# Moving the elementwise part of a chunked recurrence behind its projections, and splitting each unit of it in two

## The chip, the cores and the metric

The kernel runs on one core of one Trainium2 chip. The metric is the device time of one execution in microseconds. The core's engines are TensorE (PE in the profile), VectorE (DVE), ScalarE (ACT), GpSimd (POOL) and SyncE (SP, which here only issues DMAs). Each works through its own instructions strictly in the order in which they were laid down, and waits on semaphores for the others.

## The reference

A network of two blocks on 1024 tokens of width 1024. The change lies in the second block, in the half of its mixer that is a recurrence (RWKV) with 8 heads of 64; the other half is attention with 8 heads in three dilated patterns. Cut to what matters:

```python
proj = h @ w_in                      # rwkv columns: r, k, v, wd, ad, gd; then q, k, v of attention
p = p + (_token_shift(p) - p) * shift_mix
w_log = -softplus(-(w0 + tanh(wd) @ w_lora_up)) - 0.5
decay = exp(-exp(w_log))
a = sigmoid(a0 + ad @ a_lora_up)
kk = heads(k * k_k); kk = kk / max(norm(kk), 1e-12)
k = k * (1.0 + (a - 1.0) * k_a)
def step(state, inp):                # one token; state is 64x64 for each head
    sa = einsum('bhvk,bhk->bhv', state, -kk_t)
    state = state * w_t + sa * (kk_t * a_t) + v_t * k_t
    return state, einsum('bhvk,bhk->bhv', state, r_t)
y = group_norm(scan(step)) + sum(rh * kh * r_k) * vh     # the bonus
y_rwkv = y * g
y_attn = rmsnorm(dilated_attention(rotary(q), rotary(k), v))
x = x + concat([y_rwkv, y_attn]) @ w_out                 # then the channel mixer
```

## The kernel before

A matrix product in full precision is three products of split operands (`mm3`, L196 to L198): 128x512 outputs, 8 slices of the inner dimension, so 24 products for 512 tokens of 128 columns. The products of one column chunk land in `pm`, and VectorE scales them out into `p` (recurrence) or `at` (attention). The weights of a chunk come as `wraw` by DMA and are split by ScalarE into `whi` and by VectorE into `wlo`.

The second block's mixer is written as `lora_in`, `rotary_tables`, `attn_mask`, `out_gate`, `rkv`, `rwkv`, `attn_in`, `attn_tiles`, `attn_first`, eight calls of `rwkv_out`, `attn`, and behind it `mix_out2` and `ffn2`. The scheduler of the language turns this into one fixed order for each engine: it interleaves instructions of later parts with those of earlier ones where it sees room, in its own model of time. So attention's projections (`attn_in`, 12 column chunks, 576 products) fill TensorE between the steps of the recurrence. Only the recurrent chain's own steps have raised priority.

- `rkv` (12 column chunks): `shifted` projects, GpSimd takes the difference of neighbouring tokens, VectorE mixes (`d`). Results go to DRAM (`drkv`). For k, `removal` makes the normalised kk. For v there are transposes to `dvn`.
- `rwkv_unit(u)` for 8 units of 128 tokens: loads kk, R, K, V (tiles `pr`) through ScalarE's DMA queue, makes the decay (the lora products L1390 into `pa`, tanh, a scan L1395, exponentials, some 20 VectorE operations in all), the bonus (product L1446 with `blk`), and the products of pairs of tiles (L1429, into `pq`).
- The solver. The first of these products (`MM`, a `pr` tile, made by two VectorE multiplications of `pq` by the mask `mk`) bounces over DRAM (`dm`, 4 DMAs) into the tile `M` (4 DMAs, one buffer). GpSimd then solves 32 triangular systems by 31 substitution steps of two operations each (`fs` and `Z`). `dz` (4 DMAs out) and `xt` (4 DMAs in, one buffer) bring the solution back.
- `rwkv_maps` multiplies it in (L1479, then L1496; tiles `LR`, `KT`, `A`), and `rwkv_chain` carries the state through four steps of 32 tokens (L1524, tile `ST`), writing `dyn`. `rwkv` runs unit u, then the chain of unit u-2, then the maps of unit u-1.
- `rwkv_out` reads `dyn` back as `yn`, normalises it, and adds the bonus from `dbon`.
- Attention takes each head by the scores' products for their maxima (L1751, L1752; a reduction L1753 on VectorE; `mh` on ScalarE; `dmx` and `qm` over DRAM), the scores again, and the products with the values (L1877, into `pa`).

All `dma` calls go through SP's queue, `store` calls through ScalarE's. SP's queue is in order: a DMA whose source isn't ready holds back all that stand behind it.

Of the kernel before, what the change touches and what calls it, by code (L numbers as in the profile page):

```python
# [17 lines left out]
P = 128  # L18
# [14 lines left out]
NT = 256  # L33
# [15 lines left out]
class Build:  # L49
# [1211 lines left out]
    def lora_weights(self):  # L1261

        self.reset = self.small([P, P], tag="reset", bufs=1)
        self.nc.gpsimd.memset(self.reset, 1.0)
        self.nc.gpsimd.memset(self.reset[:, 0:P:32], 0.0)
# [53 lines left out]
    def lora_part(self, part):  # L1319

        nc = self.nc
        raw = self.small([64, NT], tag="lrw", bufs=1)
        self.dma(out=raw, in_=self.dlora[:64, NT * part:NT * part + NT])
        sl = self.small([96, 2, NT], F32R, tag="sl", bufs=1)
        nc.scalar.copy(sl[:32, 0], raw[:32])
        nc.scalar.copy(sl[64:96, 0], raw[:32])
        self.tt(sl[32:64, 0], raw[:32], sl[:32, 0].bitcast(F32), ALU.subtract)
        nc.scalar.copy(sl[32:64, 1], raw[32:])
        nc.scalar.copy(sl[64:96, 1], raw[32:])
        self.tt(sl[:32, 1], raw[32:], sl[32:64, 1].bitcast(F32), ALU.subtract)  # L1330
        return sl

    def rkv(self):
# [4 lines left out]
        for i in (1, 0, 2):  # L1338
            for j in range(4):
# [6 lines left out]
                for h in range(2):  # L1346
# [3 lines left out]
                    vn = t[:, 512 * h:512 * h + 512].rearrange("p (k v) -> p k v", v=P)  # L1350
                    self.nc.scalar.copy(vn, ps)
                    self.dma(out=self.dvn[512 * h:512 * h + 512, j].rearrange("(k t) v -> t k v", t=P), in_=vn)

# [19 lines left out]
    def rwkv_unit(self, u, sl):  # L1373

        nc, v, pool, par = self.nc, self.nc.vector, self.nc.gpsimd, self.par
        t0 = P * u
        ch = lambda t: t.rearrange("p q (c t) -> p q c t", t=32)
        tw, ta, kk = (self.slot([P, 4, P], name="pr", tag="W") for _ in range(3))
        cs, rn, K, V = (self.slot([P, 4, P], name="pr", tag="V") for _ in range(4))
        R = self.slot([P, 4, P], name="R", tag="K")  # L1380
        wd = self.small([64, 4, 4, 2], tag="wd", bufs=4)
        cols = lambda n: [(par[n] if isinstance(n, str) else n)[:, q:q + 1] for q in range(4)]
# [3 lines left out]
        own = slice(P * (u % 2), P * (u % 2) + P)  # L1386
        for q in range(4):
            ps = self.bank([P, 2, NT], "a")
            for i in range(2):
                nc.tensor.matmul(ps[:, i], self.lw[:, i, q * P:q * P + P], sl[:, i], start=True, stop=True)  # L1390
            self.act(tw[:, q], ps[:, 0, own], AF.Tanh, scale=0.5, bias=self.w0h[:, q:q + 1])
            self.act(ta[:, q], ps[:, 1, own], AF.Tanh, scale=0.5, bias=self.a0h[:, q:q + 1])
        self.ts(tw, tw, 1.0, ALU.add)
        for q in range(4):
            v.tensor_tensor_scan(out=cs[:, q], data0=self.reset, data1=tw[:, q], initial=0.0, op0=ALU.mult, op1=ALU.add)  # L1395
        rate = -0.5 * math.exp(-0.5)
        W, WI = tw, cs
        self.act(tw, cs, AF.Exp, scale=rate)
        self.act(cs, cs, AF.Exp, scale=-rate)
        for e in range(2):  # L1400
            v.tensor_copy(wd[:, :, :, e], ch(W)[64 * e:64 * e + 64, :, :, 31])

        for q, (a, b) in enumerate(zip(cols(self.ka1), cols(self.ka0))):
            self.ts(rn[:, q], ta[:, q], a, ALU.mult, b, ALU.add)
        self.stt(ta, ta, 1.0, kk, ALU.add, ALU.mult)
        self.tt(ta, ta, WI, ALU.mult)
        self.tt(ch(kk)[:, :, :, 1:], ch(kk)[:, :, :, 1:], ch(W)[:, :, :, :31], ALU.mult)
        self.tt(K, K, rn, ALU.mult)

        for q, col in enumerate(cols("r_k")):  # L1410
            self.stt(rn[:, q], R[:, q], col, K[:, q], ALU.mult, ALU.mult)
        self.tt(R, R, W, ALU.mult)
        self.tt(K, K, WI, ALU.mult)


        LR = self.slot([P, 8, 2, 96], name="LR", tag="J")
        KT = self.slot([P, 8, 96], name="KT", tag="B")
        MM = tw.rearrange("p q t -> p (q t)")[:, :256].rearrange("p (h t) -> p h t", t=32)
# [24 lines left out]
        by_tokens(ta, LR[:, :, 1, :64])  # L1443
        by_tokens(kk, LR[:, :, 0, :64])
        ps = self.q_ps([P, 4, P])
        nc.tensor.matmul(ps, self.blk, rn, start=True, stop=True)  # L1446
        self.tt(rn, ps, V, ALU.mult)
        self.store(out=self.dbon[:, :, 0, t0:t0 + P].rearrange("q p t -> p q t"), in_=rn)
        products((ta, R, LR[:, :, 1, 64:], 1), (kk, K, LR[:, :, 0, 64:], 0), (K, R, KT[:, :, 64:], 1))
        by_tokens(K, KT[:, :, :64])  # L1450
# [17 lines left out]
        return LR, KT, R, dz, wd  # L1468

    def rwkv_maps(self, unit):  # L1470

        nc = self.nc
        LR, KT, R, dz, wd = unit
# [25 lines left out]
        return maps, wd  # L1499
# [15 lines left out]
    def rwkv_chain(self, u, maps, wd):  # L1515
# [3 lines left out]
        with self.tc.high_priority():  # L1519
            for c in range(4):  # L1520
# [4 lines left out]
                if nxt is not None:  # L1525
                    self.tt(nxt[:64].rearrange("p (q e) v -> p q e v", q=4), ps[:64].rearrange("p (q e) v -> p q e v", q=4),
                            wd[:, :, c].unsqueeze(3).to_broadcast([64, 4, 2, 64]), ALU.mult)
# [641 lines left out]
```

## Time and profile before

| | |
|---|---|
| time, median of 3 runs | 3239.7 us (3235.3 to 3243.54) |
| the profiled execution's own time / its span | 3233.1 us / 3231.4 us |
| PE busy | 3009.3 us (93%), 20614 instructions |
| DVE busy | 2009.6 us (62%) |
| ACT / POOL busy | 1142.4 us (35%) / 1335.0 us (41%) |
| mean granted TensorE clock | 0.941 |
| DMA | 336.83 MB, mean 104 GB/s |
| chain that ended last, by engine | PE 61%, DVE 11%, POOL 7%, issue 5%, DMA 4%, ACT 2%, SP 2% |

The shares are averages over some 3200 us in which very different stages follow each other. The stages that the change touches lie between 1656 us (the projections of `rkv`) and about 2200 us (the first product of attention with its values). The granted clock is 1.00 at 2.4 GHz and 0.50 at 1.2 GHz.

### The profile page before, as it was taken

Reading aid. Unit: us, or ns where it says so; the run is one execution under the profiler, and the core shown is the slowest. Engines: PE = TensorE matmul, PEld = TensorE weight load, DVE = VectorE, ACT = ScalarE, POOL = GpSimd, SP = SyncE. Lnnn points to the kernel's source line nnn. Section 1 sums busy time; section 2 is a strip of 40 time slices with the busy share of each in tenths; the row PEclk is TensorE's granted clock in tenths of the full one; section 3 lists DMA queues with packets and bytes.
Section 4 is the critical chain, followed back from the end, with each engine's and each line's share of the span. In section 5 each row is a group of like instructions: output and inputs, shape, how many; then the busy total and the mean of one; then the engine's idle time right before and its main releaser. Section 6 shows DMA issues by size and latency. Waiting matters only on the chain.

```text
span 3231.4 us, 52682 instructions
## 1 busy us (share of the span) xinstructions
PE 3009.3 (93%) x20614; PEld 2678.5 (83%) x20614; DVE 2009.6 (62%) x3618; ACT 1142.4 (35%) x2168; POOL 1335.0 (41%) x1291
## 2 busy tenths in 40 slices
PE   7999999989799999999999988788988899999998
PEld 6999998979799999877877776677778788887777
DVE  7556654674676666466776555558656766664666
ACT  3344313334343333311333323424444333334111
POOL 3767310033654444232532365543214744454430
PEclk9999999989799999999899989858998899999999
DMA  5333532335222222432223554533425122224321
GB/s 148 86 94 111 174 98 59 105 101 139 78 66 79 81 82 81 150 104 74 90 95 131 146 126 112 137 99 108 115 98 196 53 85 79 80 83 174 113 85 53
DMA packets 322535, 336.83 MB, mean 104 GB/s; under 512 B 60081, under 2 KB 270734, under 8 KB 322286
## 3 DMA queue, kind: packets, MB, share of 16 engines
q1 hardware_dynamic: 289646, 310.38, 31.0%
q10 hardware_dynamic: 32640, 23.08, 2.3%
q8 instruction: 162, 2.65, 0.3%
q14 instruction: 87, 0.71, 0.1%
HBM read 232.66 MB, written 96.40 MB: 102 GB/s over the span
## 4 chain that ended last, share of the span: by engine, by line
PE 61%; DVE 11%; POOL 7%; issue 5%; DMA 4%; ACT 2%; SPq 2%; ACTq 0%; DVEq 0%; POOLq 0%
PE pm L196 13%; PE pm L197 12%; PE pm L198 12%; PE px L197 5%; PE px L196 5%; PE px L198 5%; POOL fs L149 2%; POOL Z L149 2%; DVE dn L149 2%; SPq L142 2%; PE px L292 1%; DVE t L149 1%; PE pa L1877 1%; DMA M<-dm 1%; PE pc L1604 1%
## 5 line engine op out<-in xcount | busy, mean ns | idle before, releaser
L196 PE MATMUL pm<-xh,whi 128*128 128x512 f32 (+5 forms) x1344 | 446.9, 333 | 14.2 <-DVE th L149 11.5
L198 PE MATMUL pm<-xh,wlo 128*128 128x512 f32 (+5 forms) x1344 | 446.8, 333 | 0.0
L197 PE MATMUL pm<-xl,whi 128*128 128x512 f32 (+5 forms) x1344 | 446.4, 332 | 0.0
L149 DVE TENSOR_TENSOR y<-y,pm 128x512 f32<-128x512 f32 (+1 forms) x336 | 218.1, 659 | 159.4 <-PE pm L198 159.1
L196 PE MATMUL pm<-dn,dn 128*128 128x512 f32 (+1 forms) x736 | 286.0, 389 | 6.5 <-DVE y L149 6.2
L196 PEld LDWEIGHTS pm<-xh,whi 128*128 128x128 f32 (+1 forms) x1344 | 257.8, 192 | 35.8 <-DVE th L149 12.4
L197 PE MATMUL pm<-dn,dn 128*128 128x512 f32 (+1 forms) x736 | 282.4, 384 | 1.3 <-POOL dn L149 1.3
L198 PE MATMUL pm<-dn,dn 128*128 128x512 f32 (+1 forms) x736 | 282.5, 384 | 0.0
L197 PEld LDWEIGHTS pm<-xl,whi 128*128 128x128 f32 (+1 forms) x1344 | 257.6, 192 | 19.7 <-issue 0.9
L198 PEld LDWEIGHTS pm<-xh,wlo 128*128 128x128 f32 (+1 forms) x1344 | 257.8, 192 | 19.1 <-issue 0.5
L149 POOL TENSOR_TENSOR dn<-hid,dn 128x1024 fp32r<-128x1024 f32 x44 | 131.8, 3012 | 250.9 <-ACT dn L1161 250.9
L197 PE MATMUL px<-t,sh 128*128 128x258 f32 (+2 forms) x684 | 218.7, 320 | 6.9 <-DVE t L149 6.8
L196 PE MATMUL px<-t,sh 128*128 128x258 f32 (+2 forms) x684 | 217.2, 318 | 0.4 <-DVE gt L149 0.3
L198 PE MATMUL px<-t,sl 128*128 128x258 f32 (+2 forms) x684 | 216.1, 316 | 0.0
L149 DVE TENSOR_TENSOR wlo<-wraw,whi 128x1024 fp32r<-128x1024 f32 (+2 forms) x114 | 153.9, 1351 | 76.2 <-ACT whi L170 74.7
L196 PEld LDWEIGHTS pm<-dn,dn 128*128 128x128 f32 x736 | 138.2, 188 | 43.7 <-DVE y L149 14.2
L170 ACT CAST whi<-wraw 128x1024 fp32r<-128x1024 f32 (+2 forms) x114 | 103.4, 908 | 185.7 <-PE pm L197 154.8
L197 PEld LDWEIGHTS pm<-dn,dn 128*128 128x128 f32 x736 | 138.4, 188 | 29.9 <-POOL dn L149 1.7
L198 PEld LDWEIGHTS pm<-dn,dn 128*128 128x128 f32 x736 | 138.2, 188 | 30.0
L170 ACT CAST dn<-wd 128x1024 fp32r<-128x1024 f32 x44 | 46.1, 1048 | 290.8 <-PE pm L197 290.3
L197 PEld LDWEIGHTS px<-t,sh 128*128 128x128 f32 x684 | 131.3, 192 | 17.9 <-DVE t L149 9.1
L149 POOL TENSOR_TENSOR wraw<-wraw,par 128x1024 f32<-128x1024 f32 (+1 forms) x36 | 73.4, 2041 | 169.0 <-DMA wraw<-in_w_in_dram 128.7
(600 smaller groups left out, 8788.6 us busy)
## 6 DMA issues: line engine op xcount, KB each, us to landing
wraw<-in_w_in_dram SPq DMA_DIRECT2D x61, 512.0 KB
dhid<-up SPq DMA_DIRECT2D x44, 512.0 KB
wd<-in_w_ffn_down_dram SPq DMA_DIRECT2D x44, 512.0 KB
hid<-dhid SPq DMA_DIRECT2D x44, 512.0 KB
wra<-in_w_ffn_up_dram SPq DMA_DIRECT2D x33, 512.0 KB
wrb<-in_w_ffn_up_dram SPq DMA_DIRECT2D x33, 512.0 KB
dg<-th SPq DMA_DIRECT2D x16, 514.0 KB
wraw<-in_w_out_dram SPq DMA_DIRECT2D x16, 512.0 KB
```

Of the source, the lines that this page charges most:

```text
L142: self.nc.sync.dma_start(out=out, in_=in_)
L149: (eng or self.nc.vector).tensor_tensor(out=o, in0=a, in1=b, op=op)
L170: self.nc.scalar.copy(hi, src)
L196: nc.tensor.matmul(ps, a[0], b[0], start=start, stop=False, **kw)
L197: nc.tensor.matmul(ps, a[0], b[1], start=False, stop=False, **kw)
L198: nc.tensor.matmul(ps, a[1], b[0], start=False, stop=stop, **kw)
L292: self.nc.tensor.matmul(ps[:bw, i:i + 1], src[:, i * bw:i * bw + bw], self.ones[:, 0:1], start=start and i == 0, stop=stop and i == n - 1)
L1604: nc.tensor.matmul(ps, w[:, k], (yh, yl, yh)[q][:, a:b], start=i == 0, stop=i == 11)
L1877: nc.tensor.matmul(self.po[:, i - 4 * ch], pT[:, i * P - a:i * P - a + P], self.vx[j % 2][:, k].rearrange("p e v -> p (e v)")[:, 2 * e:2 * ...
```

## The change

`rkv` runs its column chunks j outermost, in the order k, v, r within each, and calls a new `prepare(j, half)` twice for each j. It holds what was the elementwise part of `rwkv_unit`, now for one tile of 128 channels and 512 tokens instead of four of 128 channels and 128 tokens. Its results go to a new DRAM tensor `dprep`. `rwkv_unit(u)` loads them from there through SP's queue, makes the solver's product, and returns `rest`, a function with the other products and transposes; `rwkv` calls `rest` of a unit after the first part of the next one. The lora products go from 64 of 128x256 to 16 of 128x512 (L1373 in the new file), the bonus products from 8 to 8 (L1397), and V's transposed copy gets a tile of its own (`vn`). The other lines move: products L1429 to L1441, transposes L1436 to L1448, L1479 to L1494, L1496 to L1511, chain L1524 to L1539, scores L1751 and L1752 to L1765 and L1766, rwkv_out's transposes L1576 to L1590.

```diff
@@ lora_part (was: 256 tokens for two units; small tiles) @@
+    def lora_part(self, half):
+        raw = self.slot([64, 512], name="lrw", tag="V")
+        self.dma(out=raw, in_=self.dlora[:64, 512 * half:512 * half + 512])
+        sl = self.slot([96, 2, 512], F32R, "sl", "J")
@@ rkv @@
-        for i in (1, 0, 2):
-            for j in range(4):
+        self.dprep = self.dram([4, 4, P, T2], "dprep")
+        self.wd = self.small([64, 4, 32, 2], tag="wd", bufs=1)
+        sl = [self.lora_part(h) for h in range(2)]
+        for j in range(4):
+            for i in (1, 2, 0):
                 t = self.shifted(512 * i + j * P, P, self.par["mix"][:, 4 * i + j:4 * i + j + 1])
                 self.dma(out=self.drkv[i, j], in_=t)
...
-                    vn = t[:, 512 * h:512 * h + 512].rearrange("p (k v) -> p k v", v=P)
+                    vn = self.slot([P, 4, P], name="vn", tag="B")
...
+            for h in range(2):
+                self.prepare(j, h, sl[h])
+
+    def prepare(self, q, half, sl):
+        nc, v, par = self.nc, self.nc.vector, self.par
+        a, b = CH2[half]
+        ch = lambda t: t.rearrange("p (c t) -> p c t", t=32)
+        tw, ta, kk = (self.slot([P, 512], name="pr", tag="W") for _ in range(3))
+        cs, rn, K, V = (self.slot([P, 512], name="pr", tag="V") for _ in range(4))
+        R = self.slot([P, 512], name="pr", tag="K")
+        for i, t in ((3, kk), (1, K), (0, R), (2, V)):
+            self.dma(out=t, in_=self.drkv[i, q, :, a:b])
+        col = lambda n: (par[n] if isinstance(n, str) else n)[:, q:q + 1]
+        for i, (t, bias) in enumerate(((tw, self.w0h), (ta, self.a0h))):
+            ps = self.q_ps([P, 512])
+            nc.tensor.matmul(ps, self.lw[:, i, q * P:q * P + P], sl[:, i], start=True, stop=True)
+            self.act(t, ps, AF.Tanh, scale=0.5, bias=col(bias))
+        self.ts(tw, tw, 1.0, ALU.add)
+        v.tensor_tensor_scan(out=cs, data0=self.reset, data1=tw, initial=0.0, op0=ALU.mult, op1=ALU.add)
...
+        self.stt(rn, R, col("r_k"), K, ALU.mult, ALU.mult)
+        self.tt(R, R, W, ALU.mult)
+        self.tt(K, K, WI, ALU.mult)
+        for i, t in enumerate((ta, kk, R, K)):
+            self.dma(out=self.dprep[i, q, :, a:b], in_=t)
+        ps = self.q_ps([P, 512])
+        nc.tensor.matmul(ps, self.blk, rn, start=True, stop=True)
+        self.tt(rn, ps, V, ALU.mult)
+        self.dma(out=self.dbon[q, :, 0, a:b], in_=rn)
@@ rwkv_unit @@
-        for i, t in ((3, kk), (0, R), (1, K), (2, V)):
-            self.store(out=t, in_=self.drkv[i, :, :, t0:t0 + P].rearrange("q p t -> p q t"))
...
+        ta, kk, MM = (self.slot([P, 4, P], name="pr", tag="W") for _ in range(3))
+        K, R = (self.slot([P, 4, P], name="pr", tag="V") for _ in range(2))
+        for i, t in enumerate((ta, kk, R, K)):
+            self.dma(out=t, in_=self.dprep[i, :, :, t0:t0 + P].rearrange("q p t -> p q t"))
...
+        def rest():
+            LR = self.slot([P, 8, 2, 96], name="LR", tag="J")
+            KT = self.slot([P, 8, 96], name="KT", tag="B")
+            by_tokens(ta, LR[:, :, 1, :64])
+            by_tokens(kk, LR[:, :, 0, :64])
+            products((ta, R, LR[:, :, 1, 64:], 1), (kk, K, LR[:, :, 0, 64:], 0), (K, R, KT[:, :, 64:], 1))
+            by_tokens(K, KT[:, :, :64])
+            return LR, KT, R, dz
@@ rwkv @@
-                if u % 2 == 0:
-                    sl = self.lora_part(u // 2)
-                cur = self.rwkv_unit(u, sl)
+                cur = self.rwkv_unit(u)
             if prev:
+                prev = prev()
                 if last:
-                    self.rwkv_chain(u - 2, *last)
+                    self.rwkv_chain(u - 2, last)
                 last = self.rwkv_maps(prev)
```

What this does to the order on the engines, at three places. The first is TensorE between the end of the `rkv` projections and the product for unit 0's solver. Before, unit 0's solver product (L1429, two halves of the partitions, x16 each) stands at rows 10960 and 10961, the last `rkv` product at row 10864. The `pm` products between are those of `attn_in`:

```order
L196 MATMUL pm_2944_21502<-xh_16171,whi_21471 128x512
L197 MATMUL pm_2944_21502<-xl_16172,whi_21471 128x512
L198 MATMUL pm_2944_21502<-xh_16171,wlo_21472 128x512
L1429 MATMUL pq_2309_17679<-pr_17623,pr_17622 32x32 x16
L1429 MATMUL pq_2310_17697<-pr_17623,pr_17622 32x32 x16
L1390 MATMUL pa_17978<-sl_17614,lw_16410 128x256 x2
```

In the changed kernel the solver product of unit 0 (now L1441) stands at rows 11045, 11047 and 11069, with a bonus product between; the last `rkv` product is at row 10882:

```order
L196 MATMUL pm_2977_21500<-xh_16156,whi_21495 128x512
L197 MATMUL pm_2977_21500<-xl_16157,whi_21495 128x512
L1441 MATMUL pq_2399_17969<-pr_17961,pr_17960 32x32 x7
L1397 MATMUL pq_2392_17954<-pr_17922,blk_16386 128x512
L1441 MATMUL pq_2399_17969<-pr_17961,pr_17960 32x32 x9
L198 MATMUL pm_2977_21500<-xh_16156,wlo_21496 128x512
L196 MATMUL pm_2977_21500<-xh_16171,whi_21495 128x512
```

What moved: from the last `rkv` product to the end of unit 0's solver product there are now 176 products of `attn_in`, 4 lora and 3 bonus products and a group of transposes. Before, 88 of `attn_in` stood there.

The second place is SP's queue where one unit's solver hands over to the next. Before, at the hand-over from unit 0 to unit 1, `dm` and the first of the four loads of `M` stand ahead of the solution's way out, and the other three loads behind it:

```order
L142 DMA dm_18049<-pr_17955 32x8x32 x4
L142 DMA M_18180<-dm_18049 32x1024
L142 DMA dz_17950<-Z_17851 256x1x32 x4
L142 DMA M_18180<-dm_18049 32x1024 x3
L142 DMA xt_17610<-dz_17950 32x8x32 x4
```

So it stands at two hand-overs before, the first two; at the other five `dz`, `xt`, `dm` and `M` follow each other in this order. In the changed kernel the first four hand-overs have the order above, and three have the other; this is the one from unit 4 to unit 5:

```order
L142 DMA dz_19479<-Z_19380 256x1x32 x4
L142 DMA dyn_16712<-yv_19608 128x512
L142 DMA A_19678<-KT_19485 32x768 x2
L142 DMA A_19711<-KT_19485 32x768 x2
L142 DMA pr_19748<-dprep_16714 128x4x128
L142 DMA pr_19747<-dprep_16714 128x4x128
L142 DMA xt_17958<-dz_19479 32x8x32 x4
L142 DMA pr_20163<-dprep_16714 128x4x128
L142 DMA dm_19789<-pr_19746 32x8x32 x4
L142 DMA M_19794<-dm_19789 32x1024 x4
```

What moved: the split of `M` around `dz` covers four hand-overs instead of two, and in the others loads of `pr` from `dprep` now stand in the queue as well.

The third place is TensorE at the end of `attn_in`. Before, the last product of `attn_in` and the first score product of attention (L1751) stand ahead of the maps and chains of units 6 and 7 (the last product with `xt`, L1479, is at rows 11844 and 11845):

```order
L196 MATMUL pm_3008_22176<-xh_16212,whi_22145 128x512
L197 MATMUL pm_3008_22176<-xl_16213,whi_22145 128x512
L198 MATMUL pm_3008_22176<-xh_16212,wlo_22146 128x512
L1751 MATMUL pm_3023_22232<-kk_22218,qq_22217 128x256
L1496 MATMUL pm_2815_20694<-LR_19858 96x96
L1496 MATMUL pc_2816_20695<-LR_19858 96x96
L1496 MATMUL pm_2815_20694<-LR_19858 96x96
L1496 MATMUL pc_2816_20695<-LR_19858 96x96
```

In the changed kernel unit 7's products with `xt` are at rows 11636 and 11648, 125 products of `attn_in` follow, and the first head's scores (L1765) and their second part (L1766) stand behind them:

```order
L196 MATMUL pm_3030_22080<-xh_16212,whi_22049 128x512
L197 MATMUL pm_3030_22080<-xl_16213,whi_22049 128x512
L198 MATMUL pm_3030_22080<-xh_16212,wlo_22050 128x512
L1765 MATMUL pm_3045_22136<-kk_22122,qq_22121 128x256
L1794 MATMUL pq_3053_22161<-ident_66,vT_22147 128x128 x4
L1590 MATMUL pq_3081_22254<-ident_66,yn_22227 128x128 x2
L1868 MATMUL pm_3154_22581<-qq_22121,kk_22122 128x512
L1766 MATMUL pm_3045_22136<-kl_22107,qm_22110 128x256
```

What moved: the end of the recurrence now stands ahead of the end of `attn_in`, and all score products behind both. Between the products with `xt` of consecutive units there stand, in the changed kernel, 39, 11, 47, 26, 19, 16 and 26 products of `attn_in`, and the chain, maps and products of the units.

## Rows read from the trace of the kernel before

**Rows 1.** The span by lines of the chain of waits, 1780 to 2200.

```profile
by line: POOL fs L149 18.3%; POOL Z L149 17.6%; issue 9.9%; SPq L142 9.1%; DMA M<-dm 5.8%; PE pc L1524 4.0%; DMA yn<-dyn 3.7%; PE pm L198 3.4%; PE pm L196 3.4%; PE pm L197 3.4%; DMA dz<-Z 2.1%; DMA dm<-pr 1.5%; PE pq L1429 1.2%; POOL ro L14
```

**Rows 2.** Windows: us, busy of each engine (instructions), PE clock, DMA share, GB/s.

```profile
1656.00:1797.00 141.00, 137.33 (x593) 108.26 (x592) 86.49 (x91) 45.45 (x53) 39.82 (x15) 1.00 0.40 132
1797.00:2196.00 399.00, 344.58 (x4022) 291.45 (x4021) 219.65 (x516) 134.55 (x297) 201.07 (x550) 0.82 0.46 120
...
2150.00:2196.00 46.00, 42.75 (x248) 39.08 (x247) 33.02 (x107) 15.60 (x31) 9.23 (x12) 0.50 0.35 105
```

**Rows 3.** POOL's timeline: first solver step of units 0 to 2 and 7, last step.

```profile
1831.86 0.24 POOL L149 TENSOR_TENSOR fs<-Z,M 128x31 f32<-128x31 f32 x1 [32.63 <-DMA M<-dm]
...
1867.45 0.24 POOL L149 TENSOR_TENSOR fs<-Z,M 128x31 f32<-128x31 f32 x1 [3.69 <-DMA M<-dm]
...
1899.83 0.24 POOL L149 TENSOR_TENSOR fs<-Z,M 128x31 f32<-128x31 f32 x1 [1.61 <-DMA M<-dm]
...
2122.47 0.24 POOL L149 TENSOR_TENSOR fs<-Z,M 128x31 f32<-128x31 f32 x1 [10.26 <-DMA M<-dm]
...
2149.81 0.21 POOL L149 TENSOR_TENSOR Z<-Z,fs 128x8 f32<-128x8 f32 x1
```

**Rows 4.** SP's timeline at the hand-over to unit 1, and to unit 4.

```profile
1857.77 3.42 SPq L142 DMA_DIRECT2D dz<-Z  x4
1861.24 1.54 SPq L142 DMA_DIRECT2D M<-dm  x3
...
1972.33 2.55 SPq L142 DMA_DIRECT2D dz<-Z  x4
1977.39 1.82 SPq L142 DMA_DIRECT2D xt<-dz  x4
1979.25 1.93 SPq L142 DMA_DIRECT2D dm<-pr  x4
...
1982.41 2.42 SPq L142 DMA_DIRECT2D M<-dm  x4
```

**Rows 5.** VectorE's timeline at the end of the projections.

```profile
1790.51 0.69 DVE L149 TENSOR_TENSOR p<-pm,rs 128x512 f32<-128x512 f32 x1 [1.02 <-PE pm L198]
...
1796.52 0.69 DVE L149 TENSOR_TENSOR p<-pm,rs 128x512 f32<-128x512 f32 x1 [5.12 <-PE pm L198]
...
1819.61 0.58 DVE L149 TENSOR_TENSOR pr<-pq,mk 128x128 f32<-128x128 f32 x2 [1.60 <-PE pq L1429]
```

**Rows 6.** TensorE's timeline: bonus, recurrence chain, xt and map products.

```profile
1946.13 1.08 PE L1446 MATMUL pq<-pr,blk 128*128 128x512 f32 x2
...
1947.84 1.57 PE L1524 MATMUL pc<-ST,A 96*96 96x64 f32 x16
...
1952.01 1.06 PE L1479 MATMUL pc<-LR,xt 128*128 128x96 f32 x8
...
1957.15 0.24 PE L1496 MATMUL pm<-LR 32*96 32x96 f32 x1
```

**Rows 7.** VectorE's busy time in the tiles named pr alone, 1797 to 2196.

```profile
1797.00:2196.00 399.00, 84.45 (x192) 0.82 0.46 120
```

**Rows 8.** VectorE and POOL timelines: wlo beside POOL's d, and alone.

```profile
1785.38 2.91 DVE L149 TENSOR_TENSOR wlo<-wraw,whi 128x1024 fp32r<-128x1024 f32 x1 [0.20 <-ACT whi L170]
...
1811.18 1.22 DVE L149 TENSOR_TENSOR wlo<-wraw,whi 128x1024 fp32r<-128x1024 f32 x1
...
1785.32 1.89 POOL L149 TENSOR_TENSOR d<-p 128x1024 f32<-128x1024 f32 x1 [10.14 <-DVE p L149]
```

**Rows 9.** From the first head's maxima to its first product; TensorE at half clock.

```profile
2152.54 0.27 ACT L159 ACTIVATE mh<-pm 8x128 fp32r<-8x128 f32 x1
...
2158.72 0.39 SPq L142 DMA_DIRECT2D qm<-dmx  x1
...
2195.27 0.63 PE L1751 MATMUL pm<-kk,qq 128*128 128x512 f32 x1
...
2196.13 0.41 PE L1877 MATMUL pa<-vx,pT 128*128 128x128 f32 x1
```

More of the change, by code (lines that the diff above doesn't have):

```diff
@@ L1261, in lora_weights @@
     def lora_weights(self):
[L1263 removed]
+        self.reset = self.small([P, 512], tag="reset", bufs=1)
         self.nc.gpsimd.memset(self.reset, 1.0)
[L1265 removed]
+        self.nc.gpsimd.memset(self.reset[:, 0:512:32], 0.0)
         lw = self.slot([96, 2, 512], F32R, "lw", "L")
@@ new lines, in prepare @@
+    def prepare(self, q, half, sl):
[14 more added lines that the diff above has]
+        v.tensor_tensor_scan(out=cs, data0=self.reset, data1=tw, initial=0.0, op0=ALU.mult, op1=ALU.add)
+        rate = -0.5 * math.exp(-0.5)
+        W, WI = tw, cs
+        self.act(tw, cs, AF.Exp, scale=rate)
+        self.act(cs, cs, AF.Exp, scale=-rate)
+        for e in range(2):
+            v.tensor_copy(self.wd[:, q, 16 * half:16 * half + 16, e], ch(W)[64 * e:64 * e + 64, :, 31])
+        self.ts(rn, ta, col(self.ka1), ALU.mult, col(self.ka0), ALU.add)
+        self.stt(ta, ta, 1.0, kk, ALU.add, ALU.mult)
+        self.tt(ta, ta, WI, ALU.mult)
+        self.tt(ch(kk)[:, :, 1:], ch(kk)[:, :, 1:], ch(W)[:, :, :31], ALU.mult)
+        self.tt(K, K, rn, ALU.mult)
+        self.stt(rn, R, col("r_k"), K, ALU.mult, ALU.mult)
[7 more added lines that the diff above has]
+        self.dma(out=self.dbon[q, :, 0, a:b], in_=rn)
@@ L1370, in removal, with rwkv_unit @@
         self.dma(out=self.drkv[3, j], in_=kk)
-    def rwkv_unit(self, u, sl):
-        nc, v, pool, par = self.nc, self.nc.vector, self.nc.gpsimd, self.par
+    def rwkv_unit(self, u):
+        nc, pool = self.nc, self.nc.gpsimd
         t0 = P * u
[L1377 to L1382, printed above, removed]
-        for i, t in ((3, kk), (0, R), (1, K), (2, V)):
-            self.store(out=t, in_=self.drkv[i, :, :, t0:t0 + P].rearrange("q p t -> p q t"))
[L1386 to L1418, printed above, removed]
@@ L1442, in rwkv_unit @@
             self.dma(out=dm[c].rearrange("h s t -> s h t"), in_=MM[32 * c:32 * c + 32])
[L1443 to L1450, printed above, removed]
         M = self.slot([P, 32, 32], name="M", tag="U")
@@ L1467, in rwkv_unit @@
             self.dma(out=dz.rearrange("c h (k i) t -> i (c h) k t", i=4)[i], in_=Z[32 * i:32 * i + 32])
-        return LR, KT, R, dz, wd
+        def rest():
[6 more added lines that the diff above has]
+            return LR, KT, R, dz
+        return rest
     def rwkv_maps(self, unit):
         nc = self.nc
-        LR, KT, R, dz, wd = unit
+        LR, KT, R, dz = unit
         for c in range(4):
@@ L1498, in rwkv_maps @@
                     self.tt(two[:, i, 4 * k:4 * k + 4], two[:, i, 4 * k:4 * k + 4], ps, ALU.add)
-        return maps, wd
+        return maps
     def map_ps(self, shape):
@@ L1513, in rwkv_state, with rwkv_chain @@
         return st.get(c)
-    def rwkv_chain(self, u, maps, wd):
+    def rwkv_chain(self, u, maps):
         nc = self.nc
```

9 lines of the change are left out of this document (3 added, 6 removed).

## The prediction

> **What bounds the kernel now.** I read the chain of waits over the stage of the recurrence first, because the page's shares mix it with stages that the change doesn't touch. Between 1780 and 2200 us GpSimd's two solver operations, `fs` and `Z`, carry 36% of the time, issue and SP's queue 19%, the loads of `M` 5.8%, and the products with weights about 10% [rows 1]. So here the path runs through the solver and its way in and out over DRAM, though the page calls TensorE busy. The windows say how much of it TensorE has to spare: 344.6 of 399.0 us are busy from 1797 to 2196, at a mean clock of 0.82, against 137.3 of 141.0 at full clock in the projections ahead of it [rows 2]. Third, GpSimd's timeline gives the beat. The first step of unit 0 starts at 1831.86, of unit 2 at 1899.83, of unit 7 at 2122.47, and the last step ends at 2150.0 [rows 3]. The first two cycles take 34.0 us each, the other five 44.5, and the last solve 27.5. SP's timeline says why there are two kinds. At the hand-over to unit 1 three loads of `M` follow at once behind `dz` (issued by 1862.8, solver on at 1867.45) [rows 3, 4]. At that to unit 4 SP issues `dz`, waits for it, issues `xt`, then `dm`, waits for it, and only then `M` [rows 4]: the whole trip over DRAM lies between two solves.
>
> Three distances therefore make the length of this stage: from the last projection to the first solve, seven cycles, and from the last solve to the first product of attention with its values at 2196.13 (46.1 us) [rows 9]. I take each in turn; all times go against the profiled execution's 3233.1 us, which is 6.6 under the median of 3239.7.
>
> **Way to the first solve.** One product of 128x512 takes 0.2504 us, since 24 of them lie between the last two takings out at 1790.51 and 1796.52 [rows 5]. Before, 88 products of attention stood ahead of unit 0's solver product: 1796.5 + 22.0 = 1818.5, and its masking starts at 1819.61 [rows 5], which fits. From there to the first solve are 12.25 us [rows 3, 5]. In the changed kernel three things come on top.
> - Ahead of the last `rkv` product stand 12 lora products at 0.25 and 5 bonus products at 1.08 [rows 6]: 8.4, less 0.5 for the two that stood there before, about +8.
> - VectorE has 86.5 us of work in the 141 us of projections [rows 2], and six of the eight pieces of `prepare` now come in between. Everything on `pr` tiles costs 84.45 us for eight units [rows 7], 10.6 for each; some of it is masking that stays, so six pieces are 48 to 63 us. That makes 134 to 150 of 149: VectorE is as long as TensorE, and a projection waits when a whole piece stands ahead of its taking out. The bounds are 0 and 15 (one and a half pieces late); I take +6, below the middle, because most products have a second bank to go on with.
> - Then 176 products of attention (44.1), 4 lora (1.0) and 3 bonus (3.2) stand ahead of unit 0's solver product, in place of the 88: TensorE is in order, so the product waits though its inputs may lie ready.
>
> So: 1796.5 + 8 + 6 + 48.3 + 1.1 + 12.25 = 1872.2, or **+40** on the first solve. The elementwise work that left the loop doesn't pay for this: it lay on VectorE and beside the attention products, not on the way of the solver, except in unit 0.
>
> At VectorE a row speaks of a lock. `wlo` took 2.91 us where GpSimd's `d` (1.89 us) had begun 0.06 us earlier, and 1.22 alone, 1.69 less [rows 8]. Of the 141 us GpSimd is busy 39.8 [rows 2]; if the new pieces meet it as often as chance, 63 us become 63/0.72 = 88, the demand 175 of 149, and the +6 becomes +25. This is the third rival below.
> The Trainium skill, page "SBUF — State Buffer", section "SBUF: two separate sides", says that VectorE with two SBUF inputs and GpSimd share a port pair by an exclusive lock for the whole instruction, and that the loser is fully blocked. By that rule the sum would hold the +25; by chance meetings that the in-order queues avoid, the +6. The `wlo` row agrees with the rule; whether the new pieces meet `d` no row shows.
>
> **The DMAs.** From the shapes, `prepare` loads 8.4 MB, writes 8.4 to `dprep` and 2.1 to `dbon`, 18.9 MB, about what the projections move now (132 GB/s over 141 us, at a share of 0.40 [rows 2]). The share goes to about 0.8, an estimate, under the engines' limit; I cost it at nothing, hidden behind the projections' products, and late weights would cost within the 15 above. The units' loads go from ScalarE's queue to SP's, four for each unit at about 0.4 us an issue [rows 9]: 1.6 us, inside the cycles; where two of them stand between `dz` and `xt`, up to 5 in three cycles.
>
> **Cycles.** Four hand-overs of the changed kernel have the short order and three the long one: 4 x 34.0 + 3 x 44.5 = 269.5 instead of 290.6, **-21**. Below this, seven short ones would be 238; above, seven long ones 311.5. The last solve ends at 1872.2 + 269.5 + 27.5 = 2169.2, +19.2.
>
> **Way out.** Before, the end of `attn_in` and the first scores stood ahead of the last units' recurrence and ran beside the solver. Now behind the last solve come, on in-order TensorE:
> - `dz` and `xt`: 6.9 from the first `dz` issue to the last `xt` issue [rows 4], and about 3.5 to land (an estimate, under the 4.7 from `M`'s last issue to the solver [rows 3, 4]): 10.4.
> - Unit 7's products with `xt` 2.1, maps 3.8 (64 records of 0.24, a quarter of their sum as they overlap), chain 4 x 1.57 = 6.3 [rows 6], and 125 products of attention, 31.3: 43.5.
> - TensorE comes out of a wait; before, this stretch ran at clock 0.50 throughout [rows 2]. Twenty products at twice 0.25 cost 5.
> - The first head's maxima: 24 score products 0.43 apart at half clock [rows 9], 10.3. Then `mh` to `qm` over DRAM, 6.6 from 2152.54 to the end of the issue at 2158.72 [rows 9], plus 2 to land, an estimate; then two more products, 0.9. Before, all this lay hidden in the solves of units 6 and 7.
>
> Together 78.7 instead of 46.1, **+32.6**. If other heads' scores or `attn_in` cover the maxima, 19 of it go. What follows, attention's 225 us and the channel mixer, I leave as it is.
>
> **Sum.** +19.2 + 32.6 = +51.8: 3285 on the profiled execution, 3292 on the median; I forecast 3290.
>
> **Rivals.**
> 1. *Faster: TensorE binds, not the solver.* Then the 54.4 us that TensorE idles between 1797 and 2196 [rows 2] go and 8 come on: 3187, or 3193 on the median. For it: VectorE's load leaves the loop, and four hand-overs get short. It decides from some 68 products of attention for each cycle: a short cycle has 34.0 us, of which a unit's own products take 2.1 + 3.8 + 6.3 and about 5 for the rest, an estimate; 17 us are left, at 0.25. The order has 11 to 47 in a cycle and 267 spent before the first `xt` products, so the solver keeps the lead.
> 2. *About the same: all cycles short, maxima covered.* Seven at 34.0 (-31.5) and the 18.9 of the maxima hidden: 51.8 - 50.4, 3235 or 3241. For it: a load from DRAM may be issued earlier on the chip than its place suggests when nothing ahead waits. Against it: in three hand-overs `dm` and `M` stand behind `xt`, which needs the solve.
> 3. *Slower still: VectorE binds the projections* by the lock above, +19 more: 3304, or 3311. For it: the row of `wlo`, and GpSimd's part in `removal`, now spread between the pieces.
> 4. *The change does not move what it says.* The order excludes this for TensorE and SP.
>
> **How the numbers follow.** The forecast has 0.50, with 3255 to 3320 of its own, from the 0 and 15 of the projections, 5 of SP's queue and 19 of the maxima; rival 1 has 0.13, rival 2 0.16, rival 3 0.19, anything else 0.02. The range 3230 to 3328 holds the forecast, rival 3 and most of rival 2, and leaves out rival 1. A measurement of this kernel tells 0.3%, about 10 us, from no change. Faster: rival 1 and a quarter of rival 2, 0.17. The same: half of rival 2 and the rest, 0.10. Slower: 0.73.
>
> **What would show it.** Right: the first solver step near 1872, with TensorE full of attention products ahead of it and a solver product whose inputs lay ready; then four cycles near 34 and three near 44; a clock of 0.50 in parts of the loop for lack of products; the first product with the values some 79 us behind the last solve, with 125 products of `attn_in` between. VectorE's busy time from 1656 to 1810 would be near 140, and its waits for GpSimd would tell the lock. The forecast is wrong if the first solve starts near 1840, because then the order on TensorE isn't what holds it; if cycles are long where the order is short; or if TensorE shows no idle time in the loop.

## The result, and the profile after

The changed kernel takes 3271.0 us (median of 4 runs, 3267.4 to 3275.6) against 3237.5 for the kernel before (median of 4): a ratio of 1.0101, interval 1.0081 to 1.0121, 33 us slower. Forecast were 3290 and a range of 3230 to 3328. The profiled execution's own time went from 3233.1 to 3267.4, its span from 3231.4 to 3265.6, so 34 us are to be found in the trace.

GpSimd's timeline of the changed kernel, the first step of units 0, 1, 5 and 7 and the last step, answers to [rows 3]:

```profile
1876.76 0.24 POOL L149 TENSOR_TENSOR fs<-Z,M 128x31 f32<-128x31 f32 x1 [53.28 <-DMA M<-dm]
...
1912.22 0.24 POOL L149 TENSOR_TENSOR fs<-Z,M 128x31 f32<-128x31 f32 x1 [1.47 <-DMA xt<-dz]
...
2042.55 0.24 POOL L149 TENSOR_TENSOR fs<-Z,M 128x31 f32<-128x31 f32 x1 [13.54 <-DMA M<-dm]
...
2117.96 0.24 POOL L149 TENSOR_TENSOR fs<-Z,M 128x31 f32<-128x31 f32 x1 [11.46 <-DMA M<-dm]
...
2142.21 0.21 POOL L149 TENSOR_TENSOR Z<-Z,fs 128x8 f32<-128x8 f32 x1
```

TensorE's timeline, the first score product and the first product with the values, answers to [rows 9]:

```profile
2202.27 0.28 PE L1765 MATMUL pm<-kk,qq 128*128 128x256 f32 x1
...
2227.70 0.63 PE L1891 MATMUL pa<-vx,pT 128*128 128x128 f32 x2
```

The distances of the prediction, from these lines and [rows 3, 9]:

| | before | after | difference | forecast |
|---|---|---|---|---|
| first solve starts | 1831.9 | 1876.8 | +44.9 | +40.3 |
| seven cycles | 290.6 | 241.2 | -49.4 | -21.1 |
| last solve | 27.6 | 24.5 | -3.1 | 0 |
| last solve to first product with the values | 46.1 | 85.3 | +39.2 | +32.6 |
| from there to the end | 1035.3 | 1037.9 | +2.6 | 0 |
| sum | | | +34.2 | +51.8 |

The windows (columns as in [rows 2]), of the changed kernel and then of the loop in the kernel before:

```profile
1656.00:1820.00 164.00, 153.76 (x642) 117.52 (x641) 129.39 (x167) 64.78 (x83) 41.22 (x15) 0.98 0.56 186
1820.00:1877.00 57.00, 53.70 (x341) 41.52 (x342) 35.55 (x52) 13.09 (x21) 2.52 (x2) 0.97 0.81 254
1877.00:2142.00 265.00, 222.88 (x3015) 194.28 (x3013) 77.67 (x167) 68.77 (x150) 156.22 (x527) 0.72 0.43 110
2142.00:2228.00 86.00, 77.44 (x565) 63.96 (x565) 41.76 (x118) 24.79 (x40) 18.16 (x17) 0.78 0.36 103
```

```profile
1832.00:2150.00 318.00, 266.83 (x3382) 223.94 (x3371) 165.68 (x371) 105.78 (x234) 189.81 (x539) 0.84 0.47 118
```

The loop got 53 us shorter, and TensorE is busy 44 us less in it, at a mean clock of 0.72 instead of 0.84. What it doesn't do there stands in front of the loop and behind it. Over the whole kernel TensorE is busy 25.6 us longer than before, with 48 instructions fewer (the page's first line, the table of before):

```profile
PE 3034.9 (93%) x20566; PEld 2699.0 (83%) x20566; DVE 2000.9 (61%) x3542; ACT 1132.9 (35%) x2112; POOL 1317.7 (40%) x1291
```

### The profile page after: what moved, and what is told of

It reads as the page before. It is cut to its first block, busy times and chain, and to the rows that moved or that the text cites. A ratio compares the mean times of both kernels' runs of the same rounds, so it can differ in the third digit from the quotient of the medians.

```text
span 3265.6 us, 52520 instructions
## 1 busy us (share of the span) xinstructions
PE 3034.9 (93%) x20566; PEld 2699.0 (83%) x20566; DVE 2000.9 (61%) x3542; ACT 1132.9 (35%) x2112; POOL 1317.7 (40%) x1291
## 5 line engine op out<-in xcount | busy, mean ns | idle before, releaser
L196 PE MATMUL pm<-xh,whi 128*128 128x512 f32 (+5 forms) x1344 | 454.0, 338 | 18.1 <-DVE th L149 11.1
L196 PEld LDWEIGHTS pm<-dn,dn 128*128 128x128 f32 x736 | 138.2, 188 | 44.9 <-DVE y L149 15.5
L170 ACT CAST dn<-wd 128x1024 fp32r<-128x1024 f32 x44 | 46.1, 1047 | 290.9 <-PE pm L197 290.4
L149 DVE TENSOR_TENSOR sl<-ss,sh 128x512 fp32r<-128x512 f32 x88 | 93.6, 1064 | 80.1 <-ACT sh L170 80.0
```

The source lines that it names most:

```text
L149: (eng or self.nc.vector).tensor_tensor(out=o, in0=a, in1=b, op=op)
L170: self.nc.scalar.copy(hi, src)
L196: nc.tensor.matmul(ps, a[0], b[0], start=start, stop=False, **kw)
```

## Experiments

Theory L: the cycles fell by more than forecast because VectorE's operations with two SBUF operands had blocked GpSimd's steps, and these operations are gone from the loop. Theory G: what the solver gains is lost again since the order leaves TensorE too few of attention's products in the loop. On the front, theory P (the prediction's: TensorE's order holds the first solve) stands against D, the chain of data. Each round ran the kernel before again (medians of 3233.1 to 3239.9), and a ratio is to that of its own round.

### The halves of the change

`prepare_only` calls `rest` at once; `split_only` keeps the elementwise part in the unit.

```diff
 prepare_only, against the changed kernel
+        rested = rest()            # ahead of M and the solver, as before
...
+        return rested + (dz,)
-                prev = prev()
 split_only, against the kernel before
+        def rest():                # LR, KT, by_tokens, the three other products
+                prev = prev()
```

> One half of the change alone: the elementwise part lies behind the projections, but a unit's other products and transposes come at once with its first part, as before. Theory L (a solve is longer by what VectorE's operations with two SBUF operands block of GpSimd's steps): solves without other GpSimd work take 22 to 23 us, as in the changed kernel, and not the 25.7 of before; the hand-overs go back to 14 to 19 us in most places; attention's projections end ahead of the last solve, so the way from the last solve to the first product with the values is back to 45 to 55 us; about 3262 us. Rival S (the split of the unit shortened the solve): solves of 25.7, 8 times 3.6 more, about 3290 us.

> The other half alone: the elementwise part stays in the unit (its bonus factor in another tile), the other products and transposes come behind the first part of the next unit. Theory L: solves of 25.7 us and more, with 5 to 9 steps longer than 0.45 us in each; the first solve starts near 1832 as before, since 87 products of attention stand ahead of unit 0's solver product again; time within 15 us of the kernel before. Rival S: solves of 22 us, 8 times 3.6 less, about 3208 us.

`prepare_only`: 3259.9 us, 1.0071 (1.0055 to 1.0087). Its first solve is at 1881.6; the two solves without other GpSimd work take 23.3 and 24.0, two with 1 us of it at their end 22.4 and 23.5, where 22 to 23 were expected; the way out is 55.1. `split_only`: 3252.5, 1.0052 (1.0035 to 1.0069), 19 us over the kernel before where at most 15 were expected. First solve at 1832.6; five of its six solves without other work take 23.9 to 26.7, with 2 to 9 long steps in each. So each half alone is slower than before, the front's 45 us belong to the elementwise part, and so does the short solve: all solver steps sum to 147.6 us in `prepare_only`, 166.2 in `split_only`, 167.6 before. What the split alone costs stands in its hand-overs, 116.5 us in sum for 96.3 before; why they got longer was not settled. Theory L gave the right place for both, though the solves of `split_only` are shorter than the 25.7 expected.

### The lock by itself

```diff
         products((ta, kk, MM, 2))
+        psd = self.bank([P, 4, P], "a")
+        for q in range(4):
+            nc.tensor.transpose(psd[:, q], ta[:, q], self.ident)
+        dum = self.slot([P, 4, P], name="dum", tag="K")
+        for n in range(12):
+            self.tt(dum, ta, kk, ALU.mult)      # two_sbuf; in one_psum: (dum, psd, kk)
```

> The changed kernel with twelve multiplications of 128x512 more in each unit on VectorE, both operands in SBUF, into a tile that nobody reads (and four transposes into an idle bank of PSUM). Theory L: where they lie beside a solve, its steps of 0.3 us grow to 0.6 to 1.3 us in 5 or more places and the solve goes from 22.1 to 25 us or more, about a microsecond for every two of them. Rival N (the solve got shorter for another reason, fewer DMAs of ScalarE's queue or the order on GpSimd): 22.1 us stays.

> The same twelve multiplications of the same size, but the first operand is read from PSUM. Theory L: solves without other GpSimd work stay at 22.1 to 22.5 us with no step over 0.45 us. Rival V (any work of VectorE beside it slows the solver, by semaphores or by SBUF): 25 us or more, as with two SBUF operands.

Groups of VectorE and GpSimd (busy and mean in the solver's rows; ns min/median/max in those of `dum`). First `two_sbuf`:

```profile
L149 POOL TENSOR_TENSOR Z<-Z,fs 128x60 f32<-128x60 f32 (+24 forms) x248 | 92.2, 372 | 19.4
L149 POOL TENSOR_TENSOR fs<-Z,M 128x60 f32<-128x60 f32 (+24 forms) x248 | 88.5, 357 | 112.1 <-DMA M<-dm 88.9 <-DMA xt<-dz 4.5
...
L149 DVE TENSOR_TENSOR dum<-pr,pr x96: 669/689/2880, 1855.8 to 2116.7; 128x512 f32<-128x512 f32 x96
```

`one_psum`, where VectorE spends the same time:

```profile
L149 POOL TENSOR_TENSOR fs<-Z,M 128x60 f32<-128x60 f32 (+24 forms) x248 | 74.2, 299 | 129.2 <-DMA M<-dm 108.9 <-DMA xt<-dz 1.6
L149 POOL TENSOR_TENSOR Z<-Z,fs 128x60 f32<-128x60 f32 (+24 forms) x248 | 72.2, 291 | 19.3
...
L149 DVE TENSOR_TENSOR dum<-pa,pr x96: 672/691/693, 1866.3 to 2113.9; 128x512 f32<-128x512 f32 x96
```

The steps of the kernel before, then of the changed kernel:

```profile
L149 POOL TENSOR_TENSOR fs<-Z,M 128x60 f32<-128x60 f32 (+24 forms) x248 | 85.0, 343 | 108.2 <-DMA M<-dm 89.7
L149 POOL TENSOR_TENSOR Z<-Z,fs 128x60 f32<-128x60 f32 (+24 forms) x248 | 82.6, 333 | 19.3
...
L149 POOL TENSOR_TENSOR Z<-Z,fs 128x60 f32<-128x60 f32 (+24 forms) x248 | 74.1, 299 | 19.2
L149 POOL TENSOR_TENSOR fs<-Z,M 128x60 f32<-128x60 f32 (+24 forms) x248 | 72.1, 291 | 115.1 <-DMA M<-dm 93.1 <-DMA xt<-dz 3.2
```

The times are 3295.0 and 3278.2 us (one run each). The solver's steps sum to 180.7 us with two SBUF operands and to 146.4 with one in PSUM; before 167.6, changed kernel 146.2. In `two_sbuf` the solves with many `dum` beside them take 27.5 to 34.0 us, in `one_psum` the six without other GpSimd work 22.1 to 23.1. So it is not VectorE's work that slows the solver but its second operand from SBUF, and the 21.4 us that the steps lost from before to after are the elementwise part's. A stretch of the kernel before shows it step by step, GpSimd first, then VectorE:

```profile
1838.77 0.63 POOL L149 TENSOR_TENSOR fs<-Z,M 128x66 f32<-128x66 f32 x1
1839.48 0.64 POOL L149 TENSOR_TENSOR Z<-Z,fs 128x66 f32<-128x66 f32 x1
...
1838.44 2.21 DVE L149 TENSOR_TENSOR pr<-pr,pr 128x512 f32<-128x512 f32 x3
```

The same steps in the changed kernel, with nothing beside them:

```profile
1918.39 0.30 POOL L149 TENSOR_TENSOR fs<-Z,M 128x66 f32<-128x66 f32 x1
1918.77 0.31 POOL L149 TENSOR_TENSOR Z<-Z,fs 128x66 f32<-128x66 f32 x1
```

Beside VectorE the two steps take 0.63 and 0.64 for 0.30, and they end at 1839.40 and 1840.12, 0.16 and 0.17 us behind the ends of the first two of the three VectorE operations (1839.24 and 1839.95). This is the lock that the prediction took from the Trainium skill, page "SBUF — State Buffer", section "SBUF: two separate sides"; these runs agree with it, in the exemption of an operand that isn't in SBUF too.

### The front: products or data

`attn_ahead` calls `attn_in` ahead of `rkv`, so that none of its products is left for the front or the loop. `bonus_tile` takes `rn` from tag U. `bonus_later` takes the bonus out of `prepare`:

```diff
 attn_ahead
+        B.attn_in()
         B.rkv()
 bonus_tile
+        rn = self.slot([P, 512], name="pr", tag="U")
 bonus_later: in rest, not in prepare
+            for q in range(4):
+                self.stt(rn[:, q], R[:, q], self.par["r_k"][:, q:q + 1], K[:, q], ALU.mult, ALU.mult)
+            ps = self.q_ps([P, 4, P])
+            nc.tensor.matmul(ps, self.blk, rn, start=True, stop=True)
+            self.tt(rn, ps, V, ALU.mult)
```

> The changed kernel with attention's projections written and run ahead of those of the recurrence: no product of attention is left between the last projection of the recurrence and unit 0's solver product, nor in the loop. Theory P (the prediction's: TensorE's order holds unit 0's solver product, 176 products, 44 us): from the last taking out of the projections to the first solve 12 to 20 us, instead of 56.4. Rival D (the chain of data holds it: kk's normalisation, prepare, and three trips over DRAM): 40 to 56 us. The loop has nothing but its own products, so its cycles show what the solver and the trips over DRAM need alone: 29 to 31 where short, 37 to 42 where long. In all some 100 us slower than the changed kernel by D, 70 by P.

> The changed kernel with the tile of the bonus factor in prepare taken from the solver's buffer M, which is idle then, so that a piece of prepare no longer waits for the store of the piece before. Theory D: VectorE's 7.8 us of waits for that store and as much behind them go, the last taking out comes 5 to 12 us earlier, and the first solve by about as much. Theory P: the order has 205 products of attention ahead of unit 0's solver product in place of 176, so the first solve stays or comes up to 7 us later, measured from the last taking out.

> The changed kernel with the bonus taken out of prepare and put into rest, out of the stored R and K and a load of V for each unit. Theory (in-order VectorE, with prepare's pieces among the takings out, and TensorE waiting in order for the bonus products' operands, make the projections end late): 5 products of 1.08 us, a wait of 5 us for one of them and 1.4 us of VectorE in each of six pieces go from there; last taking out 1806 to 1812 instead of 1820.4, first solve 1860 to 1868. The solves get about 1 us longer for the operations now beside them: 3255 to 3266 us. Rival (the loads and stores of prepare, at a DMA share of 0.59, make the projections late): last taking out no earlier than the 5 us of the products, 1815 or later.

VectorE's timeline of the changed kernel, the last taking out and unit 0's masking in two halves [rows 5]:

```profile
1820.39 0.68 DVE L149 TENSOR_TENSOR p<-pm,rs 128x512 f32<-128x512 f32 x1
...
1860.22 0.28 DVE L149 TENSOR_TENSOR pr<-pq,mk 128x128 f32<-128x128 f32 x1
...
1865.26 0.29 DVE L149 TENSOR_TENSOR pr<-pq,mk 128x128 f32<-128x128 f32 x1 [1.58 <-PE pq L1441]
```

| | products of attention ahead | last `rkv` product ends | last taking out | first solve | from taking out to solve |
|---|---|---|---|---|---|
| changed kernel | 176 | 1813.3 | 1820.4 | 1876.8 | 56.4 |
| attn_ahead | 0 | 1946.2 | 1948.6 | 2004.9 | 56.3 |
| bonus_tile | 205 | 1815.7 | 1822.7 | 1887.8 | 65.1 |
| bonus_later | 127 | 1808.0 | 1808.0 | 1856.0 | 48.0 |

The taking out is VectorE's, and in the changed kernel it comes 7.1 us behind TensorE's last `rkv` product; meanwhile TensorE goes on with 24 products of attention. TensorE's rows there: the last `rkv` product, then the start of the first half of unit 0's solver product and its second half, without idle time ahead of either. The last line has the semaphore instructions of L1441 from 1850 to 1880; the first, for the operands' loads, is through at 1854.5:

```profile
1812.89 0.40 PE L198 MATMUL pm<-xh,wlo 128*128 128x512 f32 x1
...
1858.06 0.32 PE L1441 MATMUL pq<-pr,pr 64*32 64x32 f32 x14
...
1864.73 0.45 PE L1441 MATMUL pq<-pr,pr 64*32 64x32 f32 x32
...
L1441 PEldq EVENT_SEMAPHORE  x3: 51/51/51, 1854.5 to 1876.8; - x3
```

So here the order holds the first half 3.6 us longer than its operands do, and the second 10.2, as P has it. But the masking ends at 1865.55, and `dm` leaves only at 1867.90, since SP's queue stood 2.3 us for the store of a bonus:

```profile
1862.42 0.80 SPq L142 DMA_DIRECT2D dbon<-pr  x1
1863.28 4.51 SPq L142 DMA_DIRECT2D pr<-dprep  x4
1867.90 1.94 SPq L142 DMA_DIRECT2D dm<-pr  x4
```

With fewer products ahead, the loads of the operands come last. TensorE stands for them in `attn_ahead` and, second row, in `bonus_later`:

```profile
1987.04 0.65 PE L1441 MATMUL pq<-pr,pr 64*32 64x32 f32 x32 [5.68 <-DMA pr<-dprep]
...
1841.76 0.75 PE L1435 MATMUL pq<-pr,pr 64*32 64x32 f32 x64 [2.97 <-DMA pr<-dprep]
```

With no product ahead the first solve comes as late behind the taking out as with 176, where P expected 12 to 20 us: in the changed kernel the order is the last limit on the solver product and SP's queue the last on `dm`, the data lie only a few us behind, and taking the order away brings nothing. More products delay the solve and fewer bring it forward, at about their own time: from the last `rkv` product, 29 more cost 8.6 us, and 49 fewer, with 3 bonus products, bring 15.5. That 56.3 and 56.4 agree so well is chance: in `attn_ahead` some 8 us on the chain of waits are head 0's (a load of 4.5, a GpSimd operation of 2.4 and VectorE's work on the maxima), which run early there; how soon the data alone would be ready stays open. Its time of 3348.2 (one run) lies nearer the sum given for P, as its cycles, with nothing else in them, take only 227 us. `bonus_tile` (3268.1, one run) was a miss: the wait for the store was not what made the projections late. What `bonus_later` removes was in part: the last taking out comes 12.4 us earlier, but TensorE's last `rkv` product only 5.3, about the time of its five bonus products. In the changed kernel TensorE stood 4.95 us for a single bonus product in TensorE's timeline:

```profile
1783.80 2.08 PE L1397 MATMUL pq<-pr,blk 128*128 128x512 f32 x2 [4.95 <-DVE pr L156]
```

But `bonus_later` takes 3279.8 us, 1.0117 (1.0088 to 1.0145), no less than the changed kernel and more than expected, though its last solve ends 22 us earlier, at 2120.0. Its windows:

```profile
1856.00:2120.00 264.00, 227.15 (x2990) 196.64 (x2988) 77.78 (x171) 69.88 (x150) 151.25 (x527) 0.72 0.42 108
2120.00:2237.00 117.00, 95.99 (x649) 77.83 (x650) 55.67 (x149) 26.22 (x42) 22.28 (x18) 0.78 0.45 123
```

The way out grew to 117 us: 179 of attention's products stand there, behind unit 7's.

### The way out

`attn_spread` writes two column chunks of `attn_in` behind each of units 1 to 5. `i_outer_spread` adds `rkv` by kinds with the bonus behind v, and a unit's R and K are loaded in `rest`. `spread_act` issues the rotary DMAs by ScalarE's queue, and `combo` is that with `bonus_later`.

```diff
 attn_spread: attn_in as a generator, one yield a column chunk
+            for _ in range((0, 2, 2, 2, 2, 2, 1, 0, 0)[u]):
+                next(self.ain)
 i_outer_spread
+        for i in (1, 0, 2):
+            for j in range(4):
...
+                if i == 0:
+                    for h in range(2):
+                        self.prepare(j, h, sl[h])
...
+                for h in range(2):
+                    self.bonus(j, h, t)
 spread_act, in rotary
+            self.store(out=a[16 * k:16 * k + 16], in_=rows[k, :16])
```

> The changed kernel with attention's projections written in among the units (two column chunks behind each of units 1 to 5, one behind unit 6), so that all 576 products stand ahead of unit 7's products with the solution. Theory (the way out is long because 125 products stand behind it): from the last solve to the first product with the values 50 to 60 us instead of 85, the seven cycles at most 10 us longer in sum, since TensorE idles there: 3245 us or less beside 3271. Rival (the products only change places: the cycles take them up one for one): 31 us more in the cycles, 3265 to 3275 us.

> Both ends mended: the projections in the old order by kinds (k, r, v, each for all channels), prepare behind each r, the bonus behind each v out of the stored results, the bonus factor without a tile of its own, and attention's projections among the units as above. Unit 0's solver product has 51 products of attention ahead of it. By the readings so far: last taking out 1815 to 1835 us, as VectorE has the same work in fewer chunks; first solve 25 to 36 us behind it; seven cycles 235 to 255 us with solves of 22; way out 50 to 60: 3205 to 3230 us, faster than the kernel before. Rival (VectorE binds the later two thirds of the projections and takes back the front): last taking out after 1840, 3240 us or more.

> As attn_spread, with the 32 small DMAs of each rotary step issued by ScalarE's queue. In attn_spread 24 of them stood between the four parts of dm in SP's in-order queue, and that hand-over took 31.9 us. Theory: this hand-over falls to 15 to 19 us, 3245 us in all. Rival: ScalarE, in order, waits with these DMAs for attention's stores and holds up the chain's copies: 3255 us or more.

> Both together: the bonus in rest, attention's projections among the units, the rotary DMAs by ScalarE's queue. If front, cycles and way out add up: about 9 us less than spread_act, 3230 to 3242 us, at the kernel before; if the rival of spread_act holds, 3250 us.

`attn_spread`: 3259.7 us, 1.0063 (1.0038 to 1.0088), where 3245 or less was expected. The way out falls from 85.3 to 45.3, below the 50 to 60 expected, but the cycles take 263.4 instead of 241.2 and the last solve, with head 0's GpSimd work in it, 34.0 instead of 24.5: 32 of 40 us are given back. One hand-over takes 31.9; SP's timeline there:

```profile
2005.13 0.32 SPq L142 DMA_DIRECT2D dm<-pr  x1
2005.97 10.38 SPq L142 DMA_DIRECT2D ro<-dqkv  x21
...
2018.73 1.29 SPq L142 DMA_DIRECT2D dm<-pr  x3
```

`i_outer_spread`: 3275.2, 1.0112 (1.0094 to 1.0129), a miss, in the time that its rival gave: the last taking out comes at 1842.5, 14 us behind the last product, and the first solve 35.2 behind it, where it was. `spread_act`: 3277.4, 1.0116 (1.0090 to 1.0142). That hand-over does fall to 19.7, and the time doesn't: others lengthen, the cycles and the last solve sum to what they were in `attn_spread`, and the first solve comes 7 us later. The time is what its rival gave; whether ScalarE's waits are the cause was not tested. `combo`: 3275.6, 1.0107 (1.0083 to 1.0132), a miss: its first product with the values is at 2213.6, but attention then takes 246 us to the last one instead of 221.5. TensorE stands idle for 42.3 us of that instead of 26.8, 19.4 instead of 5.5 of it ahead of the transposes of `rwkv_out`, for that part's steps on VectorE (`bon`) and GpSimd (`yn`), and its clock is 0.88 instead of 0.94. Why those steps come later was not settled.

### The gain kept

> prepare_only (a unit's other products at once, so that some 70 products of attention stand in each cycle) with the bonus taken out of prepare as in bonus_later. Theory G (an earlier first solve is given back behind the last solve when the order holds too few of attention's products in the loop, and kept when it holds enough): the first solve comes some 20 us earlier than in prepare_only, near 1860, the way out stays at 50 to 60 us, and the time falls by 12 to 22 us to 3238 to 3248. Rival (TensorE's work and its waits decide wherever the solver stands, so an earlier first solve never pays): 3256 us or more.

`prepare_bonus` (`prepare_only` with the bonus in `rest`) takes 3236.0 us, 0.9997 (0.9984 to 1.0010), where 3238 to 3248 were expected: no slower than before, and by the ratios 1.2% or 39 us under `bonus_later`, from which it differs only in calling `rest` at once. Its first solve is at 1853.4, its way out 45 us. The windows:

```profile
1806.00:1853.00 47.00, 45.21 (x442) 36.59 (x441) 30.56 (x48) 17.89 (x26) 5.28 (x2) 0.96 0.77 247
1853.00:2143.00 290.00, 252.57 (x3264) 212.75 (x3264) 100.14 (x215) 79.39 (x160) 169.05 (x536) 0.83 0.51 133
2143.00:2188.00 45.00, 41.04 (x255) 38.30 (x256) 35.37 (x119) 15.55 (x31) 9.51 (x10) 0.58 0.35 102
```

The loop is 26 us longer than in `bonus_later` and TensorE is busy 25 us longer in it, at a clock of 0.83 instead of 0.72; between the products with `xt` of units 0 and 7 the order has 333 products of attention instead of 138, so none is left for the way out; that is 48 a cycle, not the 70 expected. Theory G held in these four kernels: an earlier first solve pays when the loop holds the products (24 us from `prepare_only` to here), and doesn't when they stand behind it (none from the changed kernel to `bonus_later`). It isn't the whole rule. In `combo` the first solve comes 24 us earlier than in `spread_act`, 288 products stand between the same two places and none behind, and the time is the same (1.0107 and 1.0116).

## Why the prediction was right, and where its steps were not

**Direction and sum.** Slower was right; 52 us were forecast and 34 came. The cycles and the last solve came 31 us better than forecast, the other distances 14 worse.

**Way to the first solve.** +44.9 for +40.3, and near the forecast in its parts if they are taken where the prediction has them, in TensorE's order. The last `rkv` product ends at 1813.3 for 1796.5 before, 16.8 later: 8 of work and 8.8 in place of the 6 taken for VectorE's term. In the window, to set against the first line of [rows 2]:

```profile
1656.00:1813.30 157.30, 147.54 (x614) 112.79 (x614) 123.62 (x161) 61.92 (x80) 38.59 (x14) 0.98 0.58 192
```

TensorE idles 9.8 us in it for 3.7 before, and 4.95 of them are the wait for one bonus product. From that last product to the masking of the second half it was 52.0 us for the 49.4 of the sum, and from there to the solve 11.5 for 12.25. The taking out came 23.9 us later than before, but as the prediction expected of the second bank, TensorE hardly waited for it (1.60 us at 1821.12). The step "TensorE is in order, so the product waits though its inputs may lie ready" held, by 3.6 us for the first half and 10.2 for the second. What it left out is how near the data come, since the last channels go through `removal`, `prepare` and three trips over DRAM: taking all these products away, in `attn_ahead`, brought nothing back, though some 8 us of another part's work stand in its way.

**Cycles: the mis-sized term.** -21.1 was forecast, -49.4 measured, and -3.1 in the last solve. The hand-overs went as forecast in sum: from the ends and starts of the solves, 96.3 to 73.8, -22.5. What the sum left out are the solves themselves, 221.9 to 191.8, -30.1, of which 21.4 are the steps, unblocked, and the rest mostly attention's GpSimd work, which no longer falls into the solves. The prediction had the lock in hand and priced it where the elementwise part goes, not where it leaves.

**Way out.** +39.2 for +32.6. To the first score product 59.9 from the last solve's end, 58.9 forecast; from there to the product with the values 25.4 for 19.8. The 5 us for a slow clock behind the wait were not measured apart; the granted clock is 0.50 from 2142 to 2160 and 1.00 from 2170 to 2202. The 125 products behind unit 7's are there, and taking them away brought 40 us.

**Rivals.** The first, that TensorE binds, was rightly put behind for the changed kernel, but its question, how many products a cycle holds, is the one that decided in `prepare_bonus`: with 333 in the seven cycles and the bonus in `rest` the elementwise part lies behind the projections at no cost, with 138 it costs 38 us. The changed kernel has 166 there by the same count; the seven numbers given with the change sum to 184, because products between the two halves of a unit's products with `xt` are in two of them. The second did not come: the maxima were not hidden. The third did not come either: over 1656 to 1820 VectorE is busy 129.4 us of 164, and its operations that took over 0.3 us more than the shortest of their shape lost 16.8 us by it, for 13.9 before the change (1656 to 1797).

## What to carry to other kernels

When work leaves a stage, ask whom it had been blocking there: a chain of short GpSimd steps beside VectorE operations with two SBUF operands was a seventh longer for it. A serial loop that gets shorter pays only if the in-order engine beside it still finds enough to do inside; count that engine's filler between the loop's steps before and after, since what doesn't fit stands behind the loop at full price. Enough filler alone didn't suffice here in `combo`. And before taking a limit away, look how close the next ones lie: here the order of TensorE, the data and SP's queue were within some 10 us of each other.

## What was not expected of the hardware

An added VectorE multiplication with both operands in SBUF cost GpSimd's chain 0.36 us on average (180.7 less 146.4 us over 96 of them, 69 beside a solve), the same one with an operand in PSUM nothing that shows. VectorE pays as well: `dum` took up to 2.88 us beside GpSimd's work with two SBUF operands, and never over 0.69 with one.
